# A hybrid encoder block on one core: low parts last in the first units, pooled products inside the next unit, token copies and one split moved

## The chip, the core and the metric

One core of a Trainium2 chip runs the whole kernel. Its engines are TensorE (PE; its weight loads stand apart as PEld), VectorE (DVE), ScalarE (ACT), GpSimd (POOL) and SyncE (SP), each with its own instruction queue that it works through in order; SP, ACT and POOL also start DMAs. The metric is the device time of one execution in microseconds (us), taken as the median of several runs. Times inside the trace are microseconds from the start of its span.

## What is computed

One layer of a streaming encoder over 512 tokens of width 1024, in float32. Cut to what the change touches:

```python
h = rms_norm(x, g_mix_pre)
(lru_x, lru_gate, pool_in, q, k, v, q_idx, k_idx, w_idx, gate_logits) = split_columns(h @ w_in)
yb = multiscale_pool(pool_in)     # 4 groups of 128: (trailing mean - token) @ w_pool[g] * pool_scale
... # a recurrence branch, a sparse attention branch, merge, out projection: x = x + ...
h = rms_norm(x, g_mem_pre); x = x + rms_norm(memory_cross_attention(h, m, w_q, w_kv, w_o))
h = rms_norm(x, g_ffn_pre)
f_gate, f_up = split(h @ w_ffn_in)
x = x + rms_norm((silu(f_gate) * f_up) @ w_ffn_out)
```

## The kernel before

**Three products for one.** Every operand of a matrix product is split into a high part (a rounded copy, made by ACT) and a low part (the rest, source minus high part, made by DVE or POOL). `mm3` (L89 to L92) multiplies high by high (L90), high weights by low activations (L91) and low weights by high activations (L92), all into one PSUM tile. The normalized input of a stage stands transposed in `hh` (high) and `hl` (low), eight feature blocks k of 128 by 512 tokens.

**Units.** A unit multiplies one 128-column weight tile with all of `hh`/`hl`: 24 matmuls of 512 columns (`unit_piece`, L406). Weights arrive by SP into six `raw` buffers, and ACT (L191) and DVE or POOL (L195, L198/L199) split them into `wh`/`wl`, of which there are four buffers each, handed out in turn: the split for unit n+4 goes into the buffer of unit n. Some units run in two column halves of 256, so that they can start when half of the tokens are turned: the first unit of all (`w0`, with only 72 columns), the first memory query unit (L1090) and the four first feed-forward units (L1300).

**Turning.** `turn_pe` transposes a token block on PE; `turn_out` (L320) copies the high part out of PSUM on ACT (L324) and then makes the low part on DVE (L325), which reads the high part.

**Pooling.** For each of four groups the loop at L679 runs a unit; `pool_block` copies the result to SBUF on ACT (L628), POOL adds it to itself with shifts (L632, L633; one to four rounds), and `finish`, run one loop step later, subtracts and splits the mean on DVE and ACT (L638, L640, L415, L416). The product with `w_pool` (three matmuls, in `product`) is run at L684 and L695, behind a whole later unit; ACT and DVE then scale it into `yb` (L648, L649). DVE in this stage also has 48 rounds of a top-k search to do in the background (L495, L496).

**Feed-forward.** The first four units are ordinary. The other products, pairs of a gate tile and an up tile, use seven products in place of eight (class `Pair`): sums of quarters of the weights (`first` to `fourth`) against sums of quarters of the tokens (`token_sums`, from `whole`, a copy of the first two token blocks that `turn_tokens` makes on ACT at L1134). `sums` and `fourth` each add one quarter to another by a DMA from POOL's queue (L1230, L1244). `fourth` splits the sum called s4 on ACT and DVE (L1212, L1215). `p6` ends with an ACT copy of one half of a PSUM tile (L1274), and `p7` writes the other half of the same tile, for which PE waits until that copy is done.

**What sets the order.** The order on each engine is laid down at build time by a scheduler that goes by the order of the code, by priorities and by its own idea of each instruction's length; instructions that are pinned keep the order of the code. On the chip every engine takes its queue strictly in that order.

Of the kernel before, what the change touches and what calls it, by code (L numbers as in the profile page):

```python
# [17 lines left out]
S = 512  # L18
KD = D // P
# [46 lines left out]
def hybrid_block_kernel(ctx: ExitStack, tc: tile.TileContext, a: dict, out: bass.AP):  # L66
    nc = tc.nc
    V, A, T, G, SP = nc.vector, nc.scalar, nc.tensor, nc.gpsimd, nc.sync
# [20 lines left out]
    def mm3(o, lh, ll, rh, rl, start, stop):  # L89
        T.matmul(o, lh, rh, start=start, stop=False, skip_group_check=True)  # L90
        T.matmul(o, lh, rl, start=False, stop=False, skip_group_check=True)  # L91
        T.matmul(o, ll, rh, start=False, stop=stop, skip_group_check=True)  # L92
# [86 lines left out]
    def low_on(engines):  # L179
        low[:] = engines  # L180
# [40 lines left out]
    def give_w(*ws):  # L221
        for w in ws:
            w[2]()
# [40 lines left out]
    start = tc.manual_schedule()  # L264
# [4 lines left out]
    ps = PS.take([P, 8])  # L269
# [4 lines left out]
    for q in range(2):  # L274
        ps = PS.take([P, 4, P])
# [35 lines left out]
    def turn_pe(src):  # L311
        pss = []
        for q in range(2):
            ps = PS.take([P, 4, P])
            for k in range(4):
                T.transpose(ps[:, k], src[:, (4 * q + k) * P:(4 * q + k + 1) * P], ident)
            pss.append(ps)
        return pss
# [14 lines left out]
    hh, hl = HH.take([P, KD, S], F32R), HL.take([P, KD, S], F32R)  # L333
# [13 lines left out]
    pss = turn_pe(X0[0][1])  # L347
# [5 lines left out]
    pss = turn_pe(X0[1][1])  # L353
# [49 lines left out]
        V.scalar_tensor_tensor(sp2, p_, 4.0, e, op0=OP.mult, op1=OP.add)  # L403


    def unit_piece(o, w, c0, c1, ks=range(KD)):  # L406
        for k in ks:
            mm3(o[:, c0:c1], w[0][:, k], w[1][:, k], hh[:, k, c0:c1], hl[:, k, c0:c1], k == 0, k == KD - 1)

    def unit(o, w):  # L410
        unit_piece(o, w, 0, S)
        give_w(w)

    def halves(src, h, l):
        A.copy(h, src)  # L415
        V.tensor_sub(l, src, f32(h))  # L416
# [24 lines left out]
    def second_turn(t):  # L441
        turn_out(turn_pe(X0[t][1]), hh, hl, t)

    w0, w1 = take_w(0), take_w(0)
    p0, p1 = PS.take([72, S]), PS.take([P, S])
    unit_piece(p0, w0, 0, 256)
    unit_piece(p1, w1, 0, 256, range(7))
    second_turn(2)
    unit_piece(p1, w1, 0, 256, range(7, KD))
    second_turn(3)  # L450
    unit_piece(p0, w0, 256, 512)
    unit_piece(p1, w1, 256, 512)
    give_w(w0, w1)
    start.__exit__(None, None, None)
# [53 lines left out]
    for m in range(1, 4):  # L508
        w = take_w()
        ps = PS.take([P, S])  # L510
# [15 lines left out]
    w = take_w()  # L526
    ps = PS.take([P, S])
# [26 lines left out]
    for i, name in enumerate(("lru_w_a", "lru_w_x")):  # L554
        t = T2.take([P, 4, P])
# [6 lines left out]
    t = T2.take([P, 4, P])  # L562
# [99 lines left out]
    gates, pools, products = (collections.deque() for _ in range(3))  # L662

    def settle(q, depth, out=None):
        while len(q) > depth:
            r = q.popleft()()
            if out is not None:
                out.append(r)

    low_on("g")  # L670
    for m in range(4):
        w = take_w()
        ps = PS.take([P, S])
# [2 lines left out]
        gates.append(lru_block(m, ps))  # L676
        pump(800)
    low_on("v")
    for g in GROUPS:  # L679
        w = take_w()  # L680
        ps = PS.take([P, S])
        unit(ps, w)
        settle(gates, 1 if g == GROUPS[0] else 0)
        settle(products, 0)  # L684
        with tc.high_priority(offset=30):
            pools.append(pool_block(g, ps))
        settle(pools, 1, products)
        pump(1000)
    low_on("vg")
    Q = [K8.take([P, 4, S], F32R) for _ in range(2)]  # L690
    for m in range(4):
        w = take_w()
        ps = PS.take([P, S])
        unit(ps, w)
        settle(products, 0)  # L695
        stacked_queries(ps, Q, m)
        settle(pools, 0, products)
        PS.give(ps)
        if m == 1:
            lru_roots()  # L700
        pump(2300)
# [132 lines left out]
    for m in range(4):  # L834
        w = take_w()
        ps = PS.take([P, S])
# [137 lines left out]
    hh, hl = HH.take([P, KD, S], F32R), HL.take([P, KD, S], F32R)  # L974
    R = []
# [20 lines left out]
    for m in range(4):  # L996
        w = take_w()
        ps = PS.take([P, NM])
# [19 lines left out]
    for i in range(4):  # L1018
        w = take_w()
        for kk in range(2):  # L1020
            k = 2 * i + kk
# [65 lines left out]
    for h in range(4):  # L1087
        w = take_w()
        ps = PS.take([P, S])
        if h == 0:  # L1090
            for c in range(2):
                unit_piece(ps, w, c * 256, c * 256 + 256)
        for k in range(KD) if h else ():
            mm3(ps, w[0][:, k], w[1][:, k], hh[:, k], hl[:, k], k == 0, k == KD - 1)
            if k == 5:
                mem_scores(h - 1)
            if k == 5 and h >= 2:
                mem_tr(h - 2)
        give_w(w)
        halves(ps, qm[0][:, h], qm[1][:, h])  # L1100
        PS.give(ps)
# [9 lines left out]
    hh, hl = HH.take([P, KD, S], F32R), HL.take([P, KD, S], F32R)  # L1111
    R = []
# [15 lines left out]

    whole = K8.take([P, 2, 4, 256])

    def turn_tokens(t, pss):
        if t < 2:
            for q in range(2):
                A.copy(whole[:, q, :, t * P:(t + 1) * P], pss[q])  # L1134
            PS.give(*pss)
            return None
        c12, d1, d3 = (T2.take([P, 4, P]) for _ in range(3))
        A.copy(c12, pss[0])
        V.tensor_sub(d1, whole[:, 0, :, (t - 2) * P:(t - 1) * P], pss[0])
        V.tensor_sub(d3, pss[1], c12)  # L1140
        PS.give(*pss)
        return c12, d1, d3

    def last_heads():
# [3 lines left out]
    project(lambda k: om[0][:, k], lambda k: om[1][:, k], 4, 4, after_o, [  # L1148
        (0, 0), lambda: mem_av(2), lambda: mem_tr(3), (0, 1), (0, 2), last_heads, (1, 0), (0, 3),
        (1, 1), (1, 2), (1, 3), (2, 0), (2, 1), (2, 2), (2, 3), (3, 0), (3, 1), lambda: R[0].turn(turn_tokens),  # L1150
        (3, 2), lambda: R[1].turn(turn_tokens), (3, 3)])
    K8.give(*om)


# [143 lines left out]
    ws = [take_w() for _ in range(NFIRST)]  # L1298
    pss = [PS.take([P, S]) for _ in range(NFIRST)]
    for c in range(2):  # L1300
        for i in range(NFIRST):
            unit_piece(pss[i], ws[i], c * 256, c * 256 + 256)
            if c == 0 and i == 2:
                pins["on"] = True
                ds = R[2].turn(turn_tokens)
                pins["on"] = False
        if c == 0:
            pins["on"] = True
            ds3 = R[3].turn(turn_tokens)
            pins["on"] = False  # L1310
            token_sums(3, *ds3)
            token_sums(2, *ds)
            K8.give(whole)
            tokens.update(b11=quad(0, 0), b21=quad(1, 0), b22=quad(1, 1))
            scratch = K8.take([P, 2, KD, P])
            cur = Pair(NFIRST // 2)
            for f in (cur.first, cur.sums, cur.second, cur.third, cur.fourth):
                f(f in (cur.first, cur.sums))
    give_w(*ws)
    for m in range(NFIRST // 2):  # L1320
# [5 lines left out]
    old = None  # L1326
    while cur is not None:
        nxt = Pair(cur.m + 1) if cur.m + 1 < NFF else None
        if nxt is None:
            state["last"] = len(specs)  # L1330
        cur.p1()
        if nxt:
            nxt.sums()
        if old:
            old.p3()
        cur.p2()
        if old:
            old.p4()
        if nxt:
            nxt.first(old is None)  # L1340
        cur.p6()
        if nxt:
            nxt.second()
        cur.p5()
        cur.p7()
        if nxt:
            nxt.third()
            nxt.fourth()
        old, cur = cur, nxt
# [75 lines left out]
```

## Time and profile before

| | |
|---|---|
| median of 3 runs | 884.73 us (883.75 to 884.84) |
| profiled execution | 883.94 us, its span 882.0 us, mean granted TensorE clock 0.999 |
| PE matmul busy | 863.5 us, 98% of the span |
| DVE busy | 608.9 us, 69% |
| ACT, POOL busy | 399.2 us, 202.1 us |
| chain that ended last | PE 81%, DVE 12%, POOL 2%, issue 2% |

A busy share of 98% says that PE has hardly a gap. The other engines are far from full on the average, but DVE is full in one stretch (about 56 to 180 us), and there an instruction's place in its queue decides when it is done. What can be won or lost lies in PE's few gaps and in whatever new ones a changed order makes.

### The profile page before, as it was taken

The numbers are of one execution on the slowest core, as the hardware profiler recorded it, in microseconds if no ns is written. First come the engines' busy times: TensorE is split into PE (matmuls) and PEld (weight loads), VectorE is DVE, ScalarE is ACT, GpSimd is POOL, SyncE is SP. The second block draws the span as 40 slices with busy tenths as digits, with TensorE's granted clock in tenths as the row PEclk, the third lists the DMA queues.
The fourth block names the chain that finished last, engine by engine and source line by source line (L and its number), as shares of the span: only waits on it lengthen the run. The fifth ranks groups of instructions, "written<-read, shape, count | busy, mean of one in ns | idle before, by whom it ended". The sixth has DMA issues, their size and how long they took to land.

```text
span 882.0 us, 12995 instructions
## 1 busy us (share of the span) xinstructions
PE 863.5 (98%) x4932; PEld 749.8 (85%) x4932; DVE 608.9 (69%) x1092; ACT 399.2 (45%) x669; POOL 202.1 (23%) x195
## 2 busy tenths in 40 slices
PE   7999999999999999999999999899999999999997
PEld 7888778888888888888888879899999999888885
DVE  7679989964864746342796788887888787732225
ACT  5455443323654445231565554545454555522121
POOL 2322455554434423210110010211111110000000
PEclk9999999999999999999999999999999999999999
DMA  8952237242332237333255301877677765333102
GB/s 246 251 128 76 79 96 192 71 119 80 89 96 72 60 108 260 99 96 95 91 186 154 96 1 36 168 167 174 150 155 157 174 161 143 120 96 96 48 1 97
DMA packets 128443, 105.52 MB, mean 120 GB/s; under 512 B 6200, under 2 KB 112252, under 8 KB 128380
## 3 DMA queue, kind: packets, MB, share of 16 engines
q1 hardware_dynamic: 120028, 89.99, 35.8%
q0 software_dynamic: 5760, 10.49, 7.6%
q10 hardware_dynamic: 2592, 4.20, 1.4%
q8 instruction: 39, 0.64, 0.3%
q14 instruction: 24, 0.20, 0.1%
HBM read 86.31 MB, written 2.10 MB: 100 GB/s over the span
## 4 chain that ended last, share of the span: by engine, by line
PE 81%; DVE 12%; POOL 2%; issue 2%; ACT 1%; DMA 1%; ACTq 0%; DVEq 0%; POOLq 0%
PE ps L91 25%; PE ps L92 25%; PE ps L90 25%; PE ps L473 2%; DVE k L938 1%; PE ps L800 1%; DVE k L954 1%; POOL t L632 1%; DVE hl L325 1%; DVE t L577 1%; DVE work L496 1%; DVE wl L195 1%; DVE m L495 1%; DVE k L963 1%; POOL y L296 1%
## 5 line engine op out<-in xcount | busy, mean ns | idle before, releaser
L191 ACT CAST wh<-raw 128x1024 fp32r<-128x1024 f32 (+1 forms) x104 | 108.5, 1045 | 226.8 <-PE ps L92 103.5
L90 PE MATMUL ps<-hh,wh 128*128 128x512 f32 (+2 forms) x584 | 207.1, 355 | 0.0
L91 PE MATMUL ps<-hl,wh 128*128 128x512 f32 (+2 forms) x584 | 206.2, 353 | 1.0 <-DVE hl L325 1.0
L92 PE MATMUL ps<-hh,wl 128*128 128x512 f32 (+2 forms) x584 | 206.4, 353 | 0.0
L195 DVE TENSOR_TENSOR wl<-raw,wh 128x1024 fp32r<-128x1024 f32 x60 | 74.5, 1246 | 102.8 <-ACT wh L191 102.8
L91 PEld LDWEIGHTS ps<-hl,wh 128*128 128x128 f32 (+1 forms) x584 | 109.1, 187 | 17.0 <-DVE hl L325 1.4
L90 PEld LDWEIGHTS ps<-hh,wh 128*128 128x128 f32 (+1 forms) x584 | 109.2, 187 | 15.9 <-ACT hh L324 0.2
L92 PEld LDWEIGHTS ps<-hh,wl 128*128 128x128 f32 (+1 forms) x584 | 109.0, 187 | 16.0
L90 PE MATMUL ps<-k,wh 128*128 128x256 f32 (+1 forms) x368 | 114.5, 311 | 0.0
L92 PE MATMUL ps<-k,wl 128*128 128x256 f32 (+1 forms) x368 | 113.8, 310 | 0.0
L91 PE MATMUL ps<-k,wh 128*128 128x256 f32 (+1 forms) x336 | 105.1, 313 | 0.0
L198 POOL TENSOR_TENSOR wl<-raw,wh 128x512 fp32r<-128x512 f32 (+1 forms) x44 | 59.3, 1348 | 148.4 <-ACT wh L191 134.2
L296 POOL TENSOR_TENSOR y<-u,half 128x1 f32<-128x1 f32 x26 | 16.0, 619 | 301.5 <-DVE u L293 260.7
L92 PE MATMUL ps<-wh,k 128*128 128x512 f32 x192 | 75.8, 395 | 0.0
L92 PEld LDWEIGHTS ps<-k,wl 128*128 128x128 f32 x368 | 69.2, 188 | 4.4
L90 PEld LDWEIGHTS ps<-k,wh 128*128 128x128 f32 x368 | 69.3, 188 | 4.2
L1215 DVE TENSOR_TENSOR wl<-raw,wh 128x1024 fp32r<-128x1024 f32 x40 | 48.9, 1225 | 31.7 <-ACT wh L1212 29.7
L91 PE MATMUL ps<-wl,k 128*128 128x512 f32 x176 | 69.4, 394 | 0.4 <-DVE wl L195 0.4
L1212 ACT CAST wh<-raw 128x1024 fp32r<-128x1024 f32 x40 | 42.0, 1049 | 61.2 <-PE ps L91 54.9
L90 PE MATMUL ps<-wh,k 128*128 128x512 f32 x176 | 69.0, 394 | 0.0
L91 PEld LDWEIGHTS ps<-k,wh 128*128 128x128 f32 x336 | 63.2, 188 | 4.2
L199 POOL TENSOR_TENSOR wl<-raw,wh 128x512 fp32r<-128x512 f32 (+1 forms) x44 | 61.3, 1393 | 0.0
(256 smaller groups left out, 1691.0 us busy)
## 6 DMA issues: line engine op xcount, KB each, us to landing
raw<-in_w_in SPq DMA_DIRECT2D x45, 512.0 KB, 4.3
raw<-in_w_ffn_in SPq DMA_DIRECT2D x44, 512.0 KB, 4.6
raw<-in_w_ffn_out SPq DMA_DIRECT2D x22, 512.0 KB, 3.6
raw<-in_w_branch SPq DMA_DIRECT2D x12, 512.0 KB, 3.5
raw<-raw POOLq DMA_DIRECT2D x20, 256.0 KB, 3.8
raw<-k POOLq DMA_DIRECT2D x20, 256.0 KB, 3.3
k<-t SPq DMA_DIRECT2D x32, 128.0 KB, 3.0
raw<-in_w_out SPq DMA_DIRECT2D x8, 512.0 KB, 3.5
```

The source lines that it names most:

```text
L90: T.matmul(o, lh, rh, start=start, stop=False, skip_group_check=True)
L91: T.matmul(o, lh, rl, start=False, stop=False, skip_group_check=True)
L92: T.matmul(o, ll, rh, start=False, stop=stop, skip_group_check=True)
L191: copy = A.copy(h, src)
L195: V.tensor_sub(l, src, f32(h))
L198: G.tensor_sub(l[:, :c], src[:, :c], f32(h[:, :c]))
L199: G.tensor_sub(l[:, c:], src[:, c:], f32(h[:, c:]))
L296: G.tensor_tensor(y, u, half, op=OP.pow)
L325: queued(V.tensor_sub(hl[:, 4 * q:4 * q + 4, dst], ps, f32(h)))
L473: T.matmul(ps[:, :n], q[j][:, hp, r], k[i][:, :n], start=i == 0, stop=i == 1, skip_group_check=True)
L1212: copy = A.copy(h, src)
L1215: V.tensor_sub(l, src, f32(h))
```

## The change

Four edits. (1) `unit_piece` gets `low_last`: all products with `hh` first (high and low weights, 16 matmuls), then the 8 with `hl`; used for both halves of `w0`, for the first memory query unit and for the first of the four feed-forward units. (2) `unit_around` puts the pooled product of the group before last behind the first four of the eight feature blocks of a unit, where it stood behind the whole unit. (3) The copies of tokens into `whole` are written after the second turn of tokens (`keep_tokens`) and no longer inside each turn. (4) `fourth` of the first pair is written after `p6` in the loop and no longer before the loop, and the `sums` of the second pair are pinned.

```diff
-    def unit_piece(o, w, c0, c1, ks=range(KD)):
+    def unit_piece(o, w, c0, c1, ks=range(KD), low_last=False):
+        if low_last:
+            for k in ks:
+                for i in range(2):
+                    T.matmul(o[:, c0:c1], w[i][:, k], hh[:, k, c0:c1], start=k == 0 and i == 0, stop=False,
+                             skip_group_check=True)
+            for k in ks:
+                T.matmul(o[:, c0:c1], w[0][:, k], hl[:, k, c0:c1], start=False, stop=k == KD - 1,
+                         skip_group_check=True)
+            return
...
-    unit_piece(p0, w0, 0, 256)
+    unit_piece(p0, w0, 0, 256, low_last=True)
...
+    def unit_around(ps, w):
+        unit_piece(ps, w, 0, S, range(4))
+        settle(products, 0)
+        unit_piece(ps, w, 0, S, range(4, KD))
+        give_w(w)
     for g in GROUPS:
...
-        unit(ps, w)
+        unit_around(ps, w)
         settle(gates, 1 if g == GROUPS[0] else 0)
-        settle(products, 0)
...
-        if t < 2:
+    kept = []
+    def keep_tokens():
+        for t, pss in enumerate(kept):
             for q in range(2):
                 A.copy(whole[:, q, :, t * P:(t + 1) * P], pss[q])
             PS.give(*pss)
+    def turn_tokens(t, pss):
+        if t < 2:
+            kept.append(pss)
             return None
...
-        (3, 2), lambda: R[1].turn(turn_tokens), (3, 3)])
+        (3, 2), lambda: R[1].turn(turn_tokens), keep_tokens, (3, 3)])
...
-            unit_piece(pss[i], ws[i], c * 256, c * 256 + 256)
+            unit_piece(pss[i], ws[i], c * 256, c * 256 + 256, low_last=i == 0)
...
-            for f in (cur.first, cur.sums, cur.second, cur.third, cur.fourth):
+            for f in (cur.first, cur.sums, cur.second, cur.third):
...
-            nxt.sums()
+            nxt.sums(old is None)
...
         cur.p6()
+        if not old:
+            cur.fourth()
```

Line numbers of the new kernel are about 10 to 21 higher: its L425 and L426 are L415 and L416 of before, L638 is L628, L658 is L648, L1233 is L1212, L1295 is L1274.

PE, the pooled product of the first group (`ps_63`) and the units around it (`ps_62` is the third pool group, `ps_64` the fourth; `t_7_66` and `t_1_67` are the high and the low part of the pooled mean). Before:

```order
L91 MATMUL ps_62_1129<-hl_1_142,wh_13_1000 128x512
L92 MATMUL ps_62_1129<-hh_1_141,wl_13_1001 128x512
L90 MATMUL ps_63_1154<-t_7_66_1116,k_7_8_764 128x512
L91 MATMUL ps_63_1154<-t_1_67_1117,k_7_8_764 128x512
L92 MATMUL ps_63_1154<-t_7_66_1116,k_7_8_764 128x512
L90 MATMUL ps_64_1190<-hh_1_141,wh_14_1062 128x512
```

Now, behind the 12th of the 24 matmuls of `ps_62`:

```order
L91 MATMUL ps_62_1129<-hl_1_142,wh_13_1000 128x512
L92 MATMUL ps_62_1129<-hh_1_141,wl_13_1001 128x512
L90 MATMUL ps_63_1142<-t_7_66_1116,k_7_8_764 128x512
L91 MATMUL ps_63_1142<-t_1_67_1117,k_7_8_764 128x512
L92 MATMUL ps_63_1142<-t_7_66_1116,k_7_8_764 128x512
L90 MATMUL ps_62_1129<-hh_1_141,wh_13_1000 128x512
```

The product has moved up by 12 matmuls; the three products that follow (`ps_65`, `ps_67`, `ps_69`) have moved up in the same way. On DVE nothing has moved ahead of the instruction that makes `t_1_67`.

ACT, the same place, from the high part of the second group's mean on. Before:

```order
L415 CAST t_4_71_1174<-t_5_63_1108 128x512
L191 CAST wh_17_1240<-raw_17_884 128x1024
L628 COPY t_9_68_1160<-ps_62_1129 128x512
L648 ACTIVATE k_0_11_786<-ps_63_1154,pc 128x512
L415 CAST t_6_76_1231<-t_9_68_1160 128x512
```

Now:

```order
L425 CAST t_4_71_1174<-t_5_63_1108 128x512
L658 ACTIVATE k_0_11_786<-ps_63_1142,pc 128x512
L191 CAST wh_17_1240<-raw_17_884 128x1024
L638 COPY t_9_68_1160<-ps_62_1129 128x512
L658 ACTIVATE k_0_11_786<-ps_65_1203,pc 128x512
L425 CAST t_6_76_1231<-t_9_68_1160 128x512
```

The scaling of each product has moved up with it. The split of `wh_17`, which goes into the buffer of `wh_13` (the weights of `ps_62`), still stands ahead of the copy of `ps_62`.

ACT, the first pair of the feed-forward stage: `raw_87` holds s4 after the DMA, `k_9_69` the sums, `ps_254` the tile of p6 and p7. Before:

```order
L1267 COPY t_2_186_5223<-ps_254_5221 128x256
L1212 CAST wh_86_5253<-raw_89_4616 128x1024
L1212 CAST wh_85_5101<-raw_88_4611 128x1024
L1212 CAST t_0_182_5106<-raw_87_4605 128x512
L1212 CAST wh_87_5270<-k_9_69_5089 128x1024
L1274 COPY t_2_186_5223<-ps_254_5221 128x256
L1212 CAST wh_88_5300<-raw_90_4621 128x1024
```

Now:

```order
L1288 COPY t_4_184_5216<-ps_254_5214 128x256
L1233 CAST wh_86_5246<-raw_89_4616 128x1024
L1233 CAST wh_85_5101<-raw_88_4611 128x1024
L1233 CAST t_2_186_5264<-raw_87_4605 128x512
L1295 COPY t_4_184_5216<-ps_254_5214 128x256
L1233 CAST wh_88_5300<-raw_90_4621 128x1024
L1233 CAST wh_87_5270<-k_9_69_5089 128x1024
```

One cast of 128x1024 has moved from ahead of the copy to behind it; the split of s4 has stayed ahead of it. On DVE, the two sums of the second pair (L1226 and L1229 on `raw_90` and `raw_89`) have moved from before the token sums to behind the first pair's sums, and on POOL the second pair's first DMA from ahead of the first pair's two to behind them. The order of SP changes only in where a few weight loads stand among the small copies of the queries.

## Rows read from the trace of the kernel before

**Rows 1.** Windows: span, busy us (x instructions) of PE, PEld, DVE, ACT, POOL; PEclk, DMA share, GB/s.

```profile
66.00:95.00 29.00, 29.00 (x128) 23.57 (x127) 29.00 (x57) 16.95 (x25) 8.01 (x6) 1.00 0.23 63
560.00:566.00 6.00, 5.90 (x49) 5.90 (x50) 5.42 (x8) 2.35 (x5) 0.87 (x1) 1.00 1.11 277
565.00:875.00 310.00, 310.00 (x2118) 286.66 (x2117) 201.79 (x293) 131.33 (x187) 32.60 (x39) 1.00 0.52 126
```

**Rows 2.** Waits of PE: line waited for, us in total, times, longest us.

```profile
PE ps L91 <- DVE hl L325: 2.9, 4, 1.0
PE ps L90 <- ACT t L1274: 2.5, 1, 2.5
PE ps L91 <- DVE t L416: 1.0, 2, 0.6
```

**Rows 3.** Timeline, PE and DVE, first unit: start, us, engine, line, out<-in [idle before].

```profile
12.46 0.36 PE L90 MATMUL ps<-hh,wh 128*72 128x256 f32 x1
13.39 0.34 PE L91 MATMUL ps<-hl,wh 128*72 128x256 f32 x1 [0.57 <-DVE hl L325]
...
21.15 0.34 PE L90 MATMUL ps<-hh,wh 128*72 128x256 f32 x1
21.88 0.34 PE L91 MATMUL ps<-hl,wh 128*72 128x256 f32 x1 [0.39 <-DVE hl L325]
...
18.42 1.41 DVE L339 SCALAR_TENSOR_TENSOR k<-k,y,gb 128x512 f32<-128x512 f32 x2
```

**Rows 4.** Timeline, PE, pool stage.

```profile
98.25 0.40 PE L90 MATMUL ps<-hh,wh 128*128 128x512 f32 x1
...
103.75 0.40 PE L90 MATMUL ps<-t,k 128*128 128x512 f32 x1
104.63 0.50 PE L91 MATMUL ps<-t,k 128*128 128x512 f32 x1 [0.48 <-DVE t L416]
...
105.19 0.40 PE L90 MATMUL ps<-hh,wh 128*128 128x512 f32 x1
...
125.25 0.40 PE L90 MATMUL ps<-hh,wh 128*128 128x512 f32 x1
```

**Rows 5.** Timeline, ACT, DVE and POOL, pool stage, each engine's rows together.

```profile
101.08 0.62 ACT L415 CAST t<-t 128x512 fp32r<-128x512 f32 x1 [2.08 <-DVE t L640]
...
106.74 0.58 ACT L628 COPY t<-ps 128x512 f32<-128x512 f32 x1
...
103.90 0.67 DVE L416 TENSOR_TENSOR t<-t,t 128x512 fp32r<-128x512 f32 x1
...
115.64 0.68 DVE L416 TENSOR_TENSOR t<-t,t 128x512 fp32r<-128x512 f32 x1
...
107.40 1.04 POOL L632 TENSOR_TENSOR t<-t 128x511 f32<-128x511 f32 x1 [7.37 <-ACT t L628]
...
113.34 0.19 POOL L633 COPY t<-t 128x8 f32<-128x8 f32 x1
```

**Rows 6.** Timeline, PE, first feed-forward unit, first half.

```profile
523.52 0.38 PE L90 MATMUL ps<-hh,k 128*128 128x256 f32 x1 [0.46 <-ACT hh L324]
...
525.32 0.39 PE L91 MATMUL ps<-hl,k 128*128 128x256 f32 x1 [0.92 <-DVE hl L325]
```

**Rows 7.** Timeline, PE, ACT, POOL and DVE, first pair, each engine's rows together.

```profile
557.35 0.28 PE L92 MATMUL ps<-hh,wl 128*128 128x256 f32 x1
560.10 0.39 PE L90 MATMUL ps<-x,wh 128*128 128x256 f32 x1 [2.48 <-ACT t L1274]
...
558.22 0.62 ACT L1212 CAST t<-raw 128x512 fp32r<-128x512 f32 x1 [2.13 <-DMA raw<-k]
...
559.68 0.36 ACT L1274 COPY t<-ps 128x256 f32<-128x256 f32 x1
...
552.85 0.87 POOL L1244 DMA_DIRECT2D raw<-k  x1 [0.32 <-issue]
...
535.89 0.69 DVE L1226 TENSOR_TENSOR k<-raw 128x512 f32<-128x512 f32 x1
```

## What to expect of the change, worked out before it was run

> **What bounds the kernel now.** I read the windows first: from 565 us to the end of the matmuls PE is busy 310.00 of 310.00 us [rows 1]. There, and in most of the program, nothing but PE's own work sets the time, so what counts is how early PE gets through its few gaps. Next the waits of PE by what ended them: the low parts of a turned input cost 2.9 us in four waits, the ACT copy ahead of p7 2.5 us in one, the low part of a pooled mean 1.0 us in two [rows 2]. The edits aim at these three. Last the timeline around each gap, and there the question is always whether the awaited instruction comes earlier, or only PE comes to another place. For that one more window matters: from 66 to 95 us DVE is busy 29.00 of 29.00 us [rows 1], so in the pool stage a DVE result is late because of its place in DVE's queue, and PE's arrival does not move it.
>
> **Part 1, low parts last in the first unit.** A 72-column matmul of 256 starts every 0.12 us; the first low one starts 0.93 us behind the one before it, and in the second half 0.73 us [rows 3]. Without waits that is 0.81 + 0.61 = 1.42 us. With 16 matmuls (1.9 us) ahead of the low ones, both waits are covered: the first half would ask for `hl` at about 14.3 us. Part of the gain is lost at once: the turn of the last token block, between the halves, needs the second of two normalizing steps on DVE, which run from 18.42 to 19.83 us [rows 3]; PE now comes there at about 19.1 and ends the turn at 20.35, not 20.85. So the second half starts 0.5 us earlier and saves its own 0.61. I take **1.15 us** earlier (bounds 0.5, if the turn eats more, and 1.42). DVE's full stretch starts from a PE result, so the pool stage shifts with it. The memory query unit shows no wait for `hl` before (all four such waits are in the first unit and at the start of the feed-forward stage): 0.
>
> **Part 2, pooled products.** This is the term that decides. A matmul of 512 starts every (103.75 - 98.25) / 24 = 0.229 us [rows 4]. The first product stood at 103.75 and even there waited for its low part until 104.63 [rows 4]. Now it stands 12 matmuls earlier, at 101.0. The high part is cast from 101.08 to 101.70, the low part made from 103.90 to 104.57 [rows 5], and the order on DVE up to that instruction is unchanged. So the product's second matmul still starts at 104.63, with 12 matmuls of the unit still to do behind it: 12 x 0.229 = **2.75 us** later than before.
>
> The delay then feeds on itself. The weights of the unit are in the buffer that the split of `wh_17` needs, and this split stands on ACT ahead of the copy L628 of the unit's result. The unit now ends at 104.63 + 0.56 (the rest of the product, as from 104.63 to 105.19 before [rows 4]) + 2.75 = 107.9, its last matmul at 108.15; a cast of 0.95 later the copy starts at 109.1 and not at 106.74 [rows 5]: 2.36 late. POOL's four rounds last 107.40 to 113.53 [rows 5], so now to 115.9. DVE needed 2.8 us from there to the end of the low part (116.3 [rows 5]); the new order puts two more instructions between, some 3.2 us: 119.1. PE wants it in the middle of the next but one unit: 107.9 + 27 x 0.229 + 12 x 0.229 + 0.23 = 117.1, and before, at the unit's end, it did not wait at all. It loses 2.0 us. The fourth product goes the same way: its copy stands behind the third's high part and another split, POOL then has two halves of weights (2.6 us) and two rounds (2.4 us), and the low part comes at about 127.8 against 125.4 for PE: 2.4 us. The second product (low part at 106.7, PE at 110.7) does not wait. Laid end to end, the last unit of the row begins at 127.8 + 0.56 + 2.75 = 131.1, where it began at 125.25 [rows 4]: **5.9 us later**. Bounds: 2.75 if the first product alone pays, 8.25 if three pay in full.
>
> What hid this before? Nothing had to: behind the whole unit the low part was due 2.75 us later. Those 12 matmuls were the cover, and the edit takes it away.
>
> [...] The longest new idle stretch is 2.65 us (101.98 to 104.63). [...]
>
> **Parts 3 and 4, feed-forward.** The first half of the first unit: PE starts at 523.52 and does four matmuls until 525.32 [rows 6], where low-last can do 15: about 1.35 us ahead. The copy L1134 of the first token block still stands before the casts that PE waits for, so the start at 523.52 stays. The second half gives 0.1 more, since two token sums now stand ahead of its low part on DVE. But being ahead counts little: PE next stops at 557.35 and goes on at 560.10, when L1274 is done [rows 7], and coming 1.4 us earlier only makes that stop longer. What moves it is the chain token sums on DVE, DMA of s4 (issued 552.85, its ACT split starts 558.22), ACT copy (559.68) [rows 7]. In the new order the split of s4 still stands ahead of that copy, so the edit does not do what it seems to; yet one cast of 128x1024 between them goes: the copy follows the split after 0.52 instead of 1.46 us, 0.94 gained. And DVE has two sums fewer ahead of the chain (the one at 535.89 is one of them [rows 7]) and one other instruction more, 0.6 us net; with a bubble filled I take 0.77. PE goes on at about 558.4: **1.7 us** gained (bounds 0.9, the cast alone, and 3.75, below). The second pair's DMA now queues behind the first pair's; by my count its split is ready 0.9 us before PE asks, so nothing, or 0.5 us lost if it slips.
>
> **Sum.** -1.15 + 5.9 - 1.7 = +3.05 us. Against the profiled execution (883.94, 1.94 around its span) that is 887.0; that execution lies 0.8 below the median of 884.73, and the median is what is predicted: **887.7 us**.
>
> **Rivals.** *B, only the first product pays.* If the copy of `ps_62` does not come late (a later free place on ACT, a shorter DVE queue), the third and fourth low parts are ready before PE asks at 117.1 and 125.4. Then pool costs 2.75: -1.15 + 2.75 - 1.7 = -0.1, 884.6, not slower. For it: DVE has idle stretches from 104 us on. Against: ACT's order, which holds the copy behind a split that needs the end of the unit. It decides at whether the third low part ends before 117.1. *C, the gains do not arrive.* The start's gain dies on the way, and the second pair's late DMA costs 0.5: 5.9 - 0.9 = +5, 889.7. For it: four bounds at their bad end are not independent, since all hang on DVE. [...] *E, faster.* s4 lands 3.3 us after its issue, as most such DMAs do by the page's table of issues, and not 5.4; PE goes on at about 556.4 and gains 3.75; together with B: -1.15 + 2.75 - 3.75 = -2.2, 882.6. Against: both of the first pair's DMAs are still issued back to back.
>
> **How the numbers follow.** Forecast 0.52, B 0.20, C 0.17, D 0.04, E 0.07. A measurement of this kernel can tell about 0.2% from no change, 1.8 us here. The forecast's own spread (886.3 to 889.3) leaves 0.03 of it within 1.8; B lies within but for 0.02 on either side. Faster 0.09, same 0.20, slower 0.71. The range 884.4 to 890.0 takes in forecast, most of B and most of C, and leaves out D, E and the ends of B and C, 0.2 together.
>
> **What would show it.** In the new profile: PE's waits for DVE L426 (was L416) rise from 1.0 to some 6 us in three to four waits, the longest near 2.7, and its waits for the ACT cast L425 to about 2; the waits for DVE L325 fall from 2.9 to under 1; one wait for L1295 (was L1274) of about 2.2 remains. The first pool row to look at is the second matmul of the first product: within 1.2 us before 104.63. If it starts near 101.5, the low part came earlier than the order says and the forecast falls; if PE's waits for the third and fourth product are under 0.5 us, B holds; if the L1295 wait is gone, E; if the granted clock drops below 1.00 after 100 us, D.

## The result and the profile after

The changed kernel takes 893.9 us (889.08 to 894.71, four runs), the kernel before 884.24 in the same comparison: a ratio of 1.0096, 95% interval [1.0078, 1.0115]. The sign was forecast, the size was not: 3 us were expected and 9.7 came.

Both profiled executions can be cut at matmuls that occur in both: the small transpose behind the first units (L515, now L525), the first product with `vv` behind the pool stage (L800, now L815), the first matmul of the feed-forward stage, the first matmul of p7, the last matmul.

| stretch, us | before | after | difference | forecast |
|---|---|---|---|---|
| start to the small transpose | 33.18 | 32.85 | -0.33 | -1.15 |
| to the first `vv` product (pool stage) | 210.31 | 220.71 | +10.40 | +5.9 |
| to the first feed-forward matmul | 280.03 | 280.01 | -0.02 | 0 |
| to the first matmul of p7 | 36.58 | 36.06 | -0.52 | -1.7 |
| to the last matmul | 314.90 | 315.05 | +0.15 | 0 |

The first row counts from the start of the span; in the new trace the first unit started 0.65 us later (13.11 against 12.46 us, [rows 3]), which hides most of what its edit gained. Everything of weight is in the pool stage. First the waits of PE in the new trace (line waited for, us in total, times, longest us); they answer to [rows 2].

```profile
PE ps L91 <- DVE t L426: 4.3, 3, 2.4
...
PE ps L90 <- ACT t L425: 2.4, 3, 1.6
PE ps L90 <- ACT t L1295: 2.0, 1, 2.0
```

The waits for the two halves of a pooled mean (low part L426, high part L425) rose from 1.0 and 0.2 us to 4.3 and 2.4. Then the windows of the new trace over that stretch (columns as in [rows 1]; the number before the last two is the granted clock), and two of the kernel before.

```profile
100.00:104.00 4.00, 1.36 (x5) 0.56 (x3) 4.00 (x10) 1.91 (x3) 0.00 (x0) 1.00 0.35 120
104.00:108.00 4.00, 3.70 (x9) 3.00 (x10) 4.00 (x10) 1.29 (x2) 0.00 (x0) 0.57 0.49 132
108.00:124.00 16.00, 15.09 (x64) 11.76 (x64) 9.95 (x26) 6.19 (x8) 9.83 (x13) 1.00 0.17 43
124.00:128.00 4.00, 2.37 (x10) 1.50 (x8) 3.50 (x7) 0.98 (x2) 1.72 (x3) 1.00 0.26 90
128.00:136.00 8.00, 6.76 (x18) 5.26 (x18) 8.00 (x18) 4.80 (x8) 3.86 (x3) 0.57 0.54 133
...
130.00:134.00 4.00, 4.00 (x11) 3.15 (x10) 4.00 (x8) 2.66 (x5) 2.57 (x2) 0.50 0.61 133
```

```profile
104.00:108.00 4.00, 3.52 (x16) 2.77 (x16) 4.00 (x11) 2.65 (x4) 0.60 (x1) 1.00 0.48 133
...
128.00:136.00 8.00, 8.00 (x37) 6.62 (x36) 8.00 (x24) 4.74 (x8) 8.00 (x7) 1.00 0.48 119
```

PE has little to do from 100 to 104 and from 125.7 to 129.4 us, and behind each of these two gaps the clock is granted at 0.50 for a while (throughout from 130 to 134 us), where the kernel before had 1.00. The matmuls tell it too (timeline of PE: start, us, operation, idle before).

```profile
100.47 0.39 PE L92 MATMUL ps<-hh,wl 128*128 128x512 f32 x1
101.41 0.49 PE L90 MATMUL ps<-t,k 128*128 128x512 f32 x1 [0.55 <-ACT t L425]
104.30 0.78 PE L91 MATMUL ps<-t,k 128*128 128x512 f32 x1 [2.39 <-DVE t L426]
...
105.30 0.63 PE L90 MATMUL ps<-hh,wh 128*128 128x512 f32 x1
105.72 0.63 PE L91 MATMUL ps<-hl,wh 128*128 128x512 f32 x1
...
107.82 0.40 PE L90 MATMUL ps<-hh,wh 128*128 128x512 f32 x1
...
117.92 0.40 PE L92 MATMUL ps<-hh,wl 128*128 128x512 f32 x1
118.58 0.50 PE L90 MATMUL ps<-t,k 128*128 128x512 f32 x1 [0.26 <-ACT t L425]
119.73 0.50 PE L91 MATMUL ps<-t,k 128*128 128x512 f32 x1 [0.64 <-DVE t L426]
...
125.67 0.40 PE L92 MATMUL ps<-hh,wl 128*128 128x512 f32 x1
127.69 0.49 PE L90 MATMUL ps<-t,k 128*128 128x512 f32 x1 [1.63 <-ACT t L425]
129.43 0.80 PE L91 MATMUL ps<-t,k 128*128 128x512 f32 x1 [1.24 <-DVE t L426]
...
135.11 0.40 PE L92 MATMUL ps<-hh,wl 128*128 128x512 f32 x1
```

The fourth product before (timeline of PE):

```profile
123.04 0.40 PE L92 MATMUL ps<-hh,wl 128*128 128x512 f32 x1
123.62 0.51 PE L90 MATMUL ps<-t,k 128*128 128x512 f32 x1 [0.18 <-ACT t L415]
124.68 0.50 PE L91 MATMUL ps<-t,k 128*128 128x512 f32 x1 [0.56 <-DVE t L416]
```

The sum can be made from these rows. **Waits**, each interval less the 0.229 us of an unhindered matmul: the first product 0.71 + 2.66 = 3.37, the third 0.43 + 0.92 = 1.35, the fourth 1.79 + 1.51 = 3.30. The same intervals before were 0.65, 0 and 0.35 + 0.83 = 1.18 ([rows 4] has the first product). Net 8.02 - 1.83 = **6.2 us**. **Half clock**: from 104.30 to 107.82 eight intervals take 3.52 instead of 1.83 us, from 129.43 to 135.11 thirteen take 5.68 instead of 2.98. Together 1.69 + 2.70 = **4.4 us**. 6.2 + 4.4 = 10.6, where the table has 10.4.

The second matmul of the first product starts at 104.30, where [rows 4] has 104.63. PE came to the product 2.34 us earlier (101.41 against 103.75) and had waited 0.71 us for the high part even so; the low part came only 0.33 us earlier, by which the whole stage had started earlier.

### The profile page after: what moved, and what is told of

It is laid out like the page before. It is cut to its first block, busy times and chain, and to the rows that moved or that the text cites. A ratio compares the mean times of both kernels' runs of the same rounds, so it can differ in the third digit from the quotient of the medians.

```text
span 891.7 us, 12990 instructions
## 1 busy us (share of the span) xinstructions
PE 869.7 (98%) x4932; PEld 754.2 (85%) x4932; DVE 608.4 (68%) x1092; ACT 399.9 (45%) x669; POOL 201.1 (23%) x195
## 4 chain that ended last, share of the span: by engine, by line
PE 81%; DVE 11%; issue 3%; POOL 2%; ACT 1%; DMA 1%; ACTq 0%; DVEq 0%; POOLq 0%
PE ps L91 25%; PE ps L92 25%; PE ps L90 25%; PE ps L483 2%; DVE k L953 1%; PE ps L815 1%; DVE k L969 1%; DVE t L587 1%; PE ps L411 1%; DVE k L978 1%; DVE work L506 1%; DVE m L505 1%; PE ps L316 1%; DVE wl L195 1%; PE ps L800 1%
## 5 line engine op out<-in xcount | busy, mean ns | idle before, releaser
L90 PE MATMUL ps<-hh,wh 128*128 128x512 f32 (+1 forms) x552 | 199.4, 361 | 0.2 <-ACT wh L1233 0.2
L92 PE MATMUL ps<-hh,wl 128*128 128x512 f32 (+1 forms) x552 | 198.6, 360 | 0.0
L91 PE MATMUL ps<-hl,wh 128*128 128x512 f32 (+1 forms) x552 | 198.5, 360 | 0.0
L90 PEld LDWEIGHTS ps<-hh,wh 128*128 128x128 f32 x552 | 105.0, 190 | 16.4 <-ACT wh L1233 0.4
L92 PEld LDWEIGHTS ps<-hh,wl 128*128 128x128 f32 x552 | 104.7, 190 | 16.4
L91 PEld LDWEIGHTS ps<-hl,wh 128*128 128x128 f32 x552 | 104.7, 190 | 15.8
L1233 ACT CAST wh<-raw 128x1024 fp32r<-128x1024 f32 x40 | 42.0, 1050 | 56.6 <-PE ps L91 53.3
```

The source lines that it names most:

```text
L1233: copy = A.copy(h, src)
```

## The experiments

Three explanations stood against each other. A: the edit of the pooled products is the whole loss, and it has two terms, waits and half clock. B: the pool edit costs the 5.9 us that were forecast, and the other edits bring the rest. C: the half clock has no price of its own, since PE would else wait longer for the next input.

**One edit undone, one edit alone.** In the first kernel the products stand behind the whole unit again, in the second the kernel before gets this edit and nothing else.

```diff
     def unit_around(ps, w):
-        unit_piece(ps, w, 0, S, range(4))
-        settle(products, 0)
-        unit_piece(ps, w, 0, S, range(4, KD))
+        unit_piece(ps, w, 0, S)
         give_w(w)
+        settle(products, 0)
```

> The changed kernel with one edit undone: the pooled products stand behind the whole unit again, all other edits stay. Theory A (the whole loss is in the pool stage, 10.4 us between the two traces; the start gives 0.3 and the feed-forward stage 0.5): 884.2 - 0.8 = 883.4 us, no stretch under clock 1.00 behind 20 us. Theory B (the pool edit costs the 5.9 us that were forecast and the rest of the loss comes from the other edits): 893.9 - 5.9 = 888.0 us.

> The kernel before with the pool edit alone: products in the middle of the unit, nothing else. Theory A: 884.2 + 10.4 = 894.6 us; PE waits 7 to 8 us in the pool stage and runs about 20 matmuls at clock 0.50. Theory B: 884.2 + 5.9 = 890.1 us.

Undone: 883.81 us, ratio 0.9996 [0.9986, 1.0005], pool stage 210.33 us. Alone: 893.63 us, ratio 1.0100 [1.0087, 1.0113]. B falls: the pool edit alone makes the whole loss, and the other three edits together change nothing that the measurement can tell. In the profiled execution of the second kernel the clock fell, within the pool stage, behind the first gap only (0.59 from 104 to 108 us), and the stage took 217.89 us, 2.8 less than in the changed kernel. Its waits are the same, 8.01 us by the same intervals where the changed kernel has 8.02. Rows and a window of its fourth product:

```profile
128.41 0.50 PE L90 MATMUL ps<-t,k 128*128 128x512 f32 x1 [1.62 <-ACT t L415]
130.15 0.50 PE L91 MATMUL ps<-t,k 128*128 128x512 f32 x1 [1.24 <-DVE t L416]
130.49 0.39 PE L92 MATMUL ps<-t,k 128*128 128x512 f32 x1
```

```profile
128.00:136.00 8.00, 6.35 (x26) 4.99 (x27) 8.00 (x19) 5.90 (x10) 3.58 (x3) 1.00 0.49 117
```

The gap ahead of the fourth product is the one of the changed kernel (1.63 and 1.24 us there), and this time the clock stayed at 1.00. So the same gap can be followed by half clock or not, and with equal waits the second fall alone is nearly all of the 2.8 us (2.70 by the rows above).

**The waits filled.** Throw-away matmuls into the product's own bank are to keep PE busy where it would wait.

```diff
                 pz = PS.take([P, S])
+                for _ in range(FILL.pop(0)):
+                    T.matmul(pz[:, :P], ident, ident, start=True, stop=True)
...
+    FILL = [14, 0, 5, 14]
```

> The changed kernel with throw-away matmuls of 128 columns ahead of the first, third and fourth pooled product (14, 5 and 14 calls into the product's own bank, 2.3, 0.8 and 2.3 us of PE time at full clock), so that PE is busy while it would wait. They are shorter than the waits, 3.4, 1.5 and 3.3 us. Theory A (of the 10.4 us, 6.1 are waits and 4.2 are matmuls at half clock): the clock stays 1.00 from 100 to 140 us and the time falls by about 4.2, to 889.7 us, though PE has more to do. Theory C (the half clock costs nothing of its own, since PE would wait for DVE anyway at the next product): 893.9 us as before the filling; theory D (fillers are in the way): 895 us or more.

The time is 892.58 us, so by the total the fillers gave back 1.3 us and not the 4.2 expected. The windows of this run say why that isn't the answer:

```profile
100.00:104.00 4.00, 4.00 (x33) 3.83 (x33) 4.00 (x9) 1.32 (x3) 0.00 (x0) 1.00 0.32 82
104.00:108.00 4.00, 4.00 (x20) 3.29 (x19) 4.00 (x13) 2.28 (x4) 0.04 (x1) 1.00 0.17 51
...
124.00:128.00 4.00, 4.00 (x33) 3.83 (x33) 4.00 (x12) 3.97 (x7) 1.19 (x1) 1.00 0.00 0
128.00:136.00 8.00, 8.00 (x37) 6.54 (x36) 8.00 (x21) 4.06 (x7) 5.73 (x6) 1.00 0.57 139
```

The clock stays at 1.00 and the pool stage takes 216.71 us, 4.0 less than in the changed kernel and 6.4 more than before: the waits without the half clock. But from the first feed-forward matmul to the last one this execution takes 355.7 us where the changed kernel takes 351.1. The second pair stops ahead of its p7 for 3.3 us, behind a split of `s4` that begins 7.7 us after the issue of its DMA, and the clock falls there (0.79 from 570 to 580 us). The wait for that copy (L1298 here):

```profile
PE ps L90 <- ACT t L1298: 3.5, 2, 3.3
```

The gain of the pool stage was real in this trace and was lost in another stage.

**The products moved the other way**, to the middle of the unit after the next, 12 matmuls later than in the kernel before.

```diff
-    gates, pools, products = (collections.deque() for _ in range(3))
+    gates, pools, products, due = (collections.deque() for _ in range(4))
...
         unit_piece(ps, w, 0, S, range(4))
-        settle(products, 0)
+        settle(due, 0)
         unit_piece(ps, w, 0, S, range(4, KD))
         give_w(w)
+        due.extend(products)
+        products.clear()
...
+    settle(due, 0)
     settle(products, 0)
```

> The changed kernel with the products moved the other way: each runs in the middle of the unit after the one behind whose end it stood in the kernel before, 12 matmuls later than there instead of 12 earlier; the other edits stay. Theory A (cover is what counts: the low part of a pooled mean is ready 0.9 us after PE wants it in the kernel before, and 12 matmuls are 2.75 us): the waits for the halves of the pooled means, 1.2 us in the kernel before and about 2.0 us counted from the intervals between matmuls, go, so 883.4 - 2.0 = 881.4 us. Rival (the buffers of the means are held half a unit longer and something else waits for them, or for the products): 883.4 us or more.

881.16 us, ratio 0.9959 [0.9947, 0.9971], as expected to 0.3 us. PE never waits for a pooled mean (windows of this run), and the pool stage takes 208.25 us, 2.06 less than before. The rival, that buffers held longer cost something, does not show in the pool stage.

```profile
100.00:104.00 4.00, 4.00 (x19) 3.32 (x18) 4.00 (x7) 1.44 (x3) 0.00 (x0) 1.00 0.39 124
104.00:108.00 4.00, 4.00 (x19) 3.26 (x18) 4.00 (x11) 2.75 (x4) 1.53 (x2) 1.00 0.51 140
108.00:124.00 16.00, 16.00 (x71) 12.98 (x70) 11.36 (x31) 5.94 (x9) 11.23 (x15) 1.00 0.23 67
```

**The stop ahead of p7.** The edit of the fourth step left the split of `s4` on ACT ahead of the copy that PE waits for. Four kernels pin the copy ahead of it in the first pair: products behind the unit, half a unit later, in the middle as in the change, and in the middle with fillers.

```diff
-        def p6(self):
+        def p6(self, pin=False):
...
-            A.copy(self.v[:, HI], self.x[:, 0])
+            copy = A.copy(self.v[:, HI], self.x[:, 0])
+            if pin:
+                tc.keep_in_program_order(copy)
...
-        cur.p6()
+        cur.p6(not old)
         if not old:
-            cur.fourth()
+            cur.fourth(True)
```

> Products behind the whole unit, the other edits kept, and one more: in the first pair the ACT copy of p6's result is held ahead of the split of s4 (both are pinned in that order), which the edit of the fourth step did not reach by itself. Theory A (PE's stop ahead of p7 lasts as long as the DMA of s4 takes to land, because the copy stands behind its split; nothing else is late there): the stop of 2.1 us falls to about 0.6, and the half clock that some executions show behind it goes: 883.8 - 1.5 = 882.3 us, down to 881 with the clock. Rival (s4 is needed soon anyway, and the wait only moves to its own product p3 in the next pair): 883.8 us.

> Products in the middle of the unit after the next, and the copy of p6 pinned ahead of the split of s4. The two gains lie in different stages, so they should add: 881.2 - 1.5 to 2.8 = 878.4 to 879.7 us. Rival (wait moves to p3): 881.2 us.

> The changed kernel with the copy of p6 pinned ahead of the split of s4, the base for the run with fillers beside it, since the DMA of s4 disturbs the feed-forward stage from run to run. Pool stage as in the changed kernel: 220 to 221 us from the second turn to the first product with vv when the clock falls twice, 218 when it falls once. Time: 893.9 - 1.5 = 892.4 us, down to 891.

> The same with the throw-away matmuls ahead of the first, third and fourth product. Theory A (half clock is 3 to 4 us of the loss, waits are 6): the pool stage takes 216.7 us as in the first run with fillers, with the clock at 1.00, and now the whole time shows it: 3 to 4 us under the run without fillers, 888 to 889.5 us. Theory C (the half clock costs nothing of its own): the same time as without fillers, 891 to 892.4 us.

| products | pool stage, us | to p7, us | p7 to the last matmul, us | time, us | ratio |
|---|---|---|---|---|---|
| behind the unit, pinned | 210.30 | 33.95 | 317.73 | 883.8 | 0.9998 [0.9989, 1.0006] |
| half a unit later, pinned | 208.21 | 33.95 | 317.37 | 880.56 | 0.9957 [0.9945, 0.9969] |
| middle, pinned | 220.77 | 33.95 | 317.13 | 891.09 | 1.0077 [1.0057, 1.0097] |
| middle, fillers, pinned | 216.67 | 33.97 | 320.10 | 892.2 | 1.0090 [1.0077, 1.0103] |

In all four the stop is gone: 33.95 us to p7 where the changed kernel takes 36.06. In the first, second and fourth the time is that of the same kernel without the pin, within 0.6 us; the third is 2.8 us faster than the changed kernel, and its runs spread from 889 to 895 (below). Of the 1.5 us or more that was expected of the pin, the first two kernels show 0.0 and 0.6. The rival was right that the wait moves, though not to p3: it moves to p7 of the second pair. One row of the waits and four of ACT in the run with the products behind the unit (L1294 is the copy here, L1232 a split):

```profile
PE ps L90 <- ACT t L1294: 1.8, 1, 1.8
```

```profile
564.49 0.62 ACT L1232 CAST t<-raw 128x512 fp32r<-128x512 f32 x1 [3.24 <-DMA raw<-k]
565.01 1.04 ACT L1232 CAST wh<-raw 128x1024 fp32r<-128x1024 f32 x1
567.75 1.04 ACT L1232 CAST wh<-k 128x1024 fp32r<-128x1024 f32 x1 [1.69 <-DVE k L1249]
568.70 0.36 ACT L1294 COPY t<-ps 128x256 f32<-128x256 f32 x1
```

ACT waits 3.24 us for the DMA of the second pair's `s4` and, one split on, 1.69 us for a sum on DVE, and the copy stands behind both. Fillers and no fillers can't be told apart by these totals, and 892.2 us is C's number and not A's 888 to 889.5. The traces say why: the fillers hold the clock in the pool stage again (1.00 from 96 to 136 us, and 216.67 against 220.77 us), and the second pair's stop takes 3 us back (2.7 us of wait, its DMA landing 7.1 us after the issue).

**Both pairs pinned**, with `s4` of the second pair also split after its own p6.

```diff
...
+        early = cur.m < NFIRST // 2 + 2
...
-        cur.p6(not old)
-        if not old:
+        cur.p6(early)
+        if early:
             cur.fourth(True)
         if nxt:
-            nxt.second()
+            nxt.second(early)
...
-            nxt.fourth()
+            if nxt.m >= NFIRST // 2 + 2:
+                nxt.fourth()
```

> Products in the middle of the unit after the next, and the copy of p6 pinned ahead of the split of s4 in the second pair too, whose s4 now is also split after its own p6. Theory (with the first pair alone pinned the stop only moved to the second pair, 1.9 us, where the same copy again stands behind the split of s4): both stops go, 880.6 - 1.9 = 878.7 us, or 878 with less of the half clock. Rival (the third pair or p3 takes the stop over): 880.6 us.

880.56 us, ratio 0.9949 [0.9935, 0.9962], where 878.7 was expected: no stop ahead of p7 is left, but a wait of 0.7 us for DVE appears in a later pair, and the time is that of the kernel with the first pair pinned. These two are the fastest of the kernels run, 0.4 to 0.5% ahead of the kernel before; nearly all of it is the later products, which gave 0.4% without a pin.

**Does the first delay make the others?** The forecast said so. One kernel puts only the first product in the middle of its unit, the other only the other three.

```diff
+    done = []
...
         unit_piece(ps, w, 0, S, range(4))
-        settle(products, 0)
+        if products and not done:
+            done.append(1)
+            settle(products, 0)
         unit_piece(ps, w, 0, S, range(4, KD))
         give_w(w)
+        settle(products, 0)
```

(The second kernel has `if done:` in the middle and fills `done` at the end of the unit.)

> The changed kernel with the first pooled product alone in the middle of its unit and the other three behind their whole units; read by its pool stage (210.3 us with all products behind, 220.7 with all in the middle and two drops of the clock). Theory A (each early product pays for its own missing cover): 2.75 us of waits at the first product, 1.7 more if the clock falls there, nothing at the others: 213.1 to 214.8 us. Theory F (as forecast, the delay of the first makes the third and the fourth late): the fourth, which had no cover to spare, waits longer too and the stage takes 1 to 2 us more, 214 to 216.5.

> The opposite: the first pooled product behind its whole unit, the other three in the middle of theirs. Theory F (the later waits come from the first one's delay): the third and the fourth wait no longer than before, the stage takes 210.3 us. Theory A (each pays for its own cover): the third asks 2.75 us earlier than before and waits some 2.0, the fourth then as much as is left of its 2.75, so 213.0 us at full clock, up to 216 if the clock falls behind one of the two waits.

The first alone: pool stage 213.07 us, 886.93 us in all, ratio 1.0028 [1.0018, 1.0038]. The others alone: 214.67 us, 890.35 us in all, ratio 1.0062 [1.0040, 1.0083]. Waits of PE from 95 to 140 us, of the first kernel, then of the second:

```profile
PE ps L91 <- DVE t L426: 2.4, 1, 2.4
PE ps L90 <- ACT t L425: 0.6, 1, 0.6
```

```profile
PE ps L91 <- DVE t L426: 2.2, 3, 1.2
PE ps L90 <- ACT t L425: 1.4, 2, 1.2
```

With the first product early and the others not, nobody waits but the first: even the 1.2 us that the fourth cost in the kernel before are covered, since PE comes later. With the first product at its old place, the third waits longer (1.37 + 0.72 = 2.09 us by the intervals) than it did in the changed kernel (1.35). So a delay of the first product shortens the third's wait. Each early product pays for the cover that it lost itself.

The second of these kernels shows one thing more. The clock fell there behind the third product, and nine intervals from 116.78 to 120.42 us took 3.64 instead of 2.06 us. A window, two rows of PE and two of ACT (the high parts of the third and the fourth mean):

```profile
117.00:120.00 3.00, 3.00 (x8) 2.34 (x7) 2.72 (x8) 1.58 (x2) 2.92 (x5) 0.50 0.09 8
```

```profile
124.28 0.50 PE L90 MATMUL ps<-t,k 128*128 128x512 f32 x1 [0.21 <-ACT t L425]
126.02 0.50 PE L91 MATMUL ps<-t,k 128*128 128x512 f32 x1 [1.24 <-DVE t L426]
```

```profile
114.59 0.62 ACT L425 CAST t<-t 128x512 fp32r<-128x512 f32 x1 [5.35 <-DVE t L650]
...
123.61 0.62 ACT L425 CAST t<-t 128x512 fp32r<-128x512 f32 x1 [5.02 <-DVE t L650]
```

The fourth product waits 1.88 us here (the interval ahead of 124.28 is 0.60 us) and 3.30 in the changed kernel, though its high part is cast 9.0 us behind the third's in this run and 9.1 in the changed kernel (117.91 and 127.02 us). The slow matmuls ran while the fourth mean was being made, and the wait became shorter by 1.4 of their 1.6 us: for this fall C is right. The first fall is different, since it lies in the unit whose result starts the third mean: with the first pair pinned it was longer (14 intervals, 2.8 us), and the third's wait was 1.28 us, hardly less than 1.35. Behind the fourth product no further mean is awaited.

**The last run** puts fillers into the kernel with both pairs pinned.

> Products in the middle of their units with fillers ahead of the first, third and fourth, and the copy of p6 ahead of the split of s4 in the first two pairs, so that the stop for s4, which swallowed the gain of the fillers in the two runs before, is out of the way. The reference is the run with products in the middle of the unit after the next and the same two pairs pinned: 880.6 us at a pool stage of 208.2 us. Theory A (half clock is a term of its own): pool stage 216.7 us at clock 1.00, so 880.6 + 8.5 = 889.1 us; with the half clock of the changed kernel, 220.7 us, it would be 893.1. Theory C (what the fillers save is lost further on whatever is pinned): 892 us again.

890.46 us, ratio 1.0064 [1.0050, 1.0077]; pool stage 216.67 us, and the clock is at 1.00 in every window of 10 us up to the last matmul. That is 1.4 above what A expects and 2.6 below the 893.1 of the half clock; 893.1 is a reckoned time, the same kernel without fillers was not run. Of the 1.4, 1.2 lie behind p7 (317.55 against 316.32 us: a wait of 1.6 us for DVE in a later pair).

The runs without fillers settle it in another way. Each run has a mean granted clock, and the same kernel is faster where the clock fell less:

```
changed kernel               us     clock     changed, first pair pinned   us     clock
                           889.08   0.998                                889.07   0.999
                           893.83   0.993                                889.98   0.997
                           893.98   0.994                                890.37   0.996
                           894.71   0.993                                891.81   0.995
                                                                         893.43   0.992
                                                                         895.06   0.993
```

At 0.998 and 0.999 both take 889.1 us, at 0.992 to 0.994 they take 893.4 to 895.1. The half clock is worth 4 to 6 us of the time of one and the same program, so C falls for the changed kernel. And 889.1 is about what the kernel takes with the waits alone: 884.2 + 6.2 less 0.3 and 0.5 for the other edits is 889.6. The mean clock of a run does not say where the clock fell, and not every fall costs as much: in the kernel before and in the one with the pool edit alone, 0.004 of mean clock go with 1.7 and 1.5 us.

## Why the prediction was wrong, step by step

- **The clock, rival D (the granted clock drops in the pool stage), chance 0.04.** This is the step that failed. The argument was one row: clock 1.00 from 560 to 566 us, behind a stop of 2.48 us [rows 1, 7]. By it the sum had this term at nothing. The trace of the kernel before has 1.00 in every window of 10 us from 0 to 870 us: it showed no fall in the program, nor what one would cost. The new trace has 0.50 behind two gaps, 4.4 us. What one row could not show: the clock may or may not fall at the same gap, as at the fourth product, where it was 0.50 behind 1.63 and 1.24 us in the changed kernel and 1.00 behind 1.62 and 1.24 us with the pool edit alone. The profiled execution of the kernel before had a mean clock of 0.999. Of 58 later runs of that kernel 13 had this, with a mean time of 883.6 us, 21 had 0.997 (884.2 us) and 18 had 0.995 or 0.996 (885.3 us). The stop ahead of p7 does show a lower clock in one trace: in the run with the pool edit alone, the granted clock from 566 to 574 us, around the end of that stop at 567.99, is 0.79.
- **The pool waits, 5.9 us, measured 6.2.** Right in size: 2.75, 2.0 and 2.4 less the 1.2 that the fourth had waited before, against 3.37 - 0.65 = 2.7, 1.35 and 3.30 - 1.18 = 2.1. The sum is nearer than its parts: the third was 0.65 too long and the fourth 0.9 too short. "Those 12 matmuls were the cover" is right, and the run with 12 more matmuls of cover shows it from the other side. "The delay then feeds on itself" is wrong: the two half experiments show each wait to be the product's own. The copy of `ps_62` is late because PE is late, and then PE also asks later. The forecast's own numbers had it: without the delay the low part would end at 116.3 as before and PE would ask at 117.1 - 2.75 = 114.4, a wait of 1.9 us in place of 2.0.
- **The start, -1.15, measured -0.33 from the start of the span.** The stretch from the first 72-column matmul to the small transpose took 20.72 us before and 19.73 in the changed kernel: 0.99 gained, within the bounds of the forecast, of which the later start of the unit took 0.65 away. The gain also varies: 20.54 us in the other profile without the edit, 19.73 to 20.96, median 20.2, in twelve with it, 0.4 by the median and under the lower bound. In the new trace the first half gained 0.5 and not 0.8, because its second matmul now needs the low part of the weights and waits 0.25 us for that; the second half gained its 0.6, and the turn of the last token block took 0.1 back.
- **Feed-forward, -1.7, measured -0.5.** The kernel with the pool edit alone has the old feed-forward code, and its stretch to p7 is 36.19 us, where the kernel before has 36.58; with the edits it is 35.94 to 36.19 in five profiles without pin and fillers. So the gain is between 0 and 0.6, under the lower bound of 0.9. Rows of POOL, ACT and PE of the changed kernel, against [rows 7]:

```profile
562.89 0.89 POOL L1265 DMA_DIRECT2D raw<-k  x1
```

```profile
568.69 0.62 ACT L1233 CAST t<-raw 128x512 fp32r<-128x512 f32 x1 [2.31 <-DMA raw<-k]
569.21 0.37 ACT L1295 COPY t<-ps 128x256 f32<-128x256 f32 x1
```

```profile
569.63 0.39 PE L90 MATMUL ps<-x,wh 128*128 128x256 f32 x1 [1.96 <-ACT t L1295]
```

The cast between split and copy went, as forecast: the copy follows after 0.52 instead of 1.46 us. But the DMA of `s4` is issued 29.32 us after the first feed-forward matmul (562.89 - 533.57), and before it was 29.33 (552.85 - 523.52): the 0.77 us by which DVE was to be ahead never came. Which instruction took it back was not tried apart. And the transfer took 0.4 longer to land.
- **The rest held**: one stop of 2.0 us for L1295 remains, the waits for the low part of the turned input fell from 2.9 to 0.7, the memory query unit gave nothing.

With what was measured the sum is -0.3 + 6.2 + 4.4 - 0.5 = +9.8. Of the 6.7 us between this and the forecast, 4.4 are the clock, 2.0 the gains at the start and in the feed-forward stage that did not come, and 0.3 the pool waits. Without the clock it would have been +5.4, or 890 us, the upper end of the range.

## What to carry to other kernels

Before an instruction is moved ahead on an engine, count what stands between it and the producer of its input: that work is the cover, and each consumer loses its own. Where a low part comes late because of its producer's queue, move the consumer later, not earlier; here 12 matmuls later gave 0.4% and 12 earlier cost 1%. And price every new gap of TensorE twice, once as a wait (here 6.2 us) and once as matmuls at half clock behind it (here 4.4 us), even if one trace shows a gap that went unpunished. Where PE would have waited anyway for a result already in the making, the second price can be nearly nothing, as behind the third product of the run without the first, where 1.4 of 1.6 us came back.

## What the runs showed of the hardware

- In the changed kernel eight matmuls ran at 0.50 behind the first gap (0.55 and 2.39 us idle with one matmul between), and thirteen behind the last (1.63 and 1.24 us, again one matmul between). The gap of 0.26 and 0.64 us had no such effect there. With the pool edit alone a gap like the last (1.62 and 1.24 us) was followed by 1.00. The stop ahead of p7, 1.9 to 2.5 us in one piece, was followed by 1.00 in the kernel before (560 to 566 us) and in the changed kernel (566 to 574 us), and by a mean of 0.79 from 566 to 574 us with the pool edit alone, whose feed-forward code is that of the kernel before.
- The warm-up matmuls at the start took a different time in two profiles though the code up to them is the same: the same 30 took 4.09 us in the profile before and 5.18 in the one after (timelines of PE, before, then after), and the first unit began 0.65 us later.

```profile
5.36 4.09 PE L261 MATMUL ps<-ident 128*128 128x128 f32 x30
```

```profile
5.27 5.18 PE L261 MATMUL ps<-ident 128*128 128x128 f32 x30
```

- From the issue of the first pair's `s4` transfer to the start of its split it took 5.4 us in the profile before, 5.8 in the changed kernel, 5.0 with the pool edit alone and 4.0 with the fillers (558.41 to 562.43 us); the second pair's took up to 7.7 (564.46 to 572.11 us, in the first run with fillers). Where the copy for PE stood behind the split on ACT, as in the kernel before and in the changed one, PE's stop ended with that copy: it was done at 560.04 us and PE went on at 560.10, in the changed kernel at 569.58 and 569.63.
